# A tuned decoder layer: the norms' factors reach all partitions through device memory instead of an fp32 product with ones

## The chip, the cores and the metric

The kernel runs on one core of a Trainium2 chip. The metric is the device time of one execution in microseconds (us), lower is better. Each kernel is run several times, and the median stands for it; a profile shows one execution. Engines are named as in the profile: PE is TensorE's matrix product and PEld its loading of weights, DVE is VectorE, ACT is ScalarE, POOL is GpSimd, SP is SyncE, which here only issues DMAs.

## The reference

One layer of a hybrid decoder on a batch of one, 256 tokens, width 1024, everything in float32:

```python
h  = rms_norm(x, ln1_g)                       # x * rsqrt(mean(x*x, -1) + 1e-6) * g
q, k, v, z, xbc, dt, ga, gb = split(h @ w_in) # 1024 -> 10272 columns
y_a = moba_attention(rms(q), rms(k), v) @ w_o_attn   # 16 heads of 64; one block of 256: causal attention
y_b = mamba2_mixer(z, xbc, dt, ...) @ w_o_ssm        # conv, chunked scan (2 chunks of 128), 32 heads of 64
x  = x + (sigmoid(ga) * y_a + sigmoid(gb) * y_b) @ w_out
h2 = rms_norm(x, ln2_g)
x  = x + (silu(g_ff) * u_ff) @ w_down         # g_ff, u_ff = split(h2 @ w_gate_up), 2816 wide
h3 = rms_norm(x, ln3_g)
x  = x + (p @ w_ple_proj) * sigmoid(h3 @ w_ple_gate)
```

## The kernel before

**Products.** A float32 product is made of three products of rounded numbers: each operand is split into a high part (`wh` for weights, rounded by ACT) and a residual (`wl` = weight minus high part, by DVE, line 260), and PE computes high times high, high times residual, and residual times high. Weights stream from device memory in pieces of 512 KB, `raw` [128 partitions, 2, 512], all on SP's queue (line 272). There are 5 `raw`, 4 `wh` and 6 `wl` buffers, so a load waits until DVE has read the piece five before it, and DVE runs ahead of PE by at most six residuals.

**Stages.** The input projection runs as panels of 512 columns (`PANELS` gives the order), each 1024 deep: the class `Panel` holds activations as PE's stationary operand, with PSUM tiles `g`; the class `Rows` holds weights as the stationary operand, with tiles `gr`, for the gate and up projections of the feed-forward part. In between stand the attention, the scan, and the output projections. The sequence of the main products is fixed by the code. All else (attention scores, the scan, transposes) is *small work*: its products use PSUM tiles `pb` and are put between the main products.

**What orders the small work.** A `Filler` keeps a count `fill.now` of the nanoseconds of PE work that have been written out so far. Each piece of small work is a generator that yields the earliest count at which its next step may be written; the distances come from the table `LAG`, one number for each kind of step. After each group of main products (three in `Panel.step`) `fill.step()` runs one step that is due. The other engines' instructions follow from this at build time, in an order set by priorities: `w` (weights) ahead of `ev` (evictions) ahead of `bg` (small work). In the trace, each engine then goes through its list in order.

**The norms.** `hn`, `h2n` are normalized activations laid out with the channels on the partitions and the 256 tokens along the row; the factor of a token (`rstd1`, `rstd2`: [128 tokens, 2], made by POOL's power on line 406) is thus needed along the row, the same in every partition. `norm_task` and `norm2` do that: ACT scales the identity by the factor, once for each half of the tokens (`dg`, 2 x [128, 128]); PE multiplies a matrix of ones (`ones_m`) by it in full float32, which leaves in every partition of `pr` the 256 factors; ACT copies them to `rbc`; DVE multiplies by it, four times for the eight blocks of channels: lines 451 and 454 at the first norm, 1139 at the second, where line 1138 first adds the two parts of the residual stream. ACT then rounds the product to the high part, and DVE subtracts for the residual (lines 460 and 1142). The first panels do not need `hn`: they work on activations without the token's factor, which is applied when they are evicted. The gate and up projections need `h2n`.

Elsewhere the kernel already takes one tensor through device memory: `e1t` is written to `e1d` (line 543) and read back, repeated, as `e1c` (line 545).

Of the kernel before, what the change touches and what calls it, by code (L numbers as in the profile page):

```python
# [10 lines left out]
F32 = mybir.dt.float32  # L11
F32R = mybir.dt.float32r
AF = mybir.ActivationFunctionType
ALU = mybir.AluOpType
AX = mybir.AxisListType

P = 128
T = 256
# [16 lines left out]
    ('v', 0, 2048),  # L35
    ('v', 1, 2560),
    ('q', 1, 512),
    ('k', 0, 1024),
    ('k', 1, 1536),
    ('gb', 0, 9248),  # L40
    ('xbc', 4, 7168),
    ('xbc', 5, 7680),
# [23 lines left out]


LAG = {
    "norm": 0, "norm.x": 7982, "norm.k": 5731, "dt": 3113, "dt.t": 1660, "dt.e": 891, "dt.low": 0,
    "dt.end": 5490, "xbc": 3857, "xbc.t": 2999, "xbc.end": 16627, "z": 0, "z.t": 3129, "z.end": 768,  # L70
    "qk": 15739, "qk.t": 6258, "qk.end": 0, "v": 1782, "cb": 3077, "rows": 0, "prep": 877, "seg": 102,
    "seg.next": 9127, "out": 8638, "out.xdt": 352, "out.end": 545, "off": 3241, "off.end": 51, "finish": 4321,
    "finish.ones": 8093, "sc": 1152, "sc.tr": 1416, "tr": 2000, "tr.val": 0, "val": 5094, "val.end": 1076,
    "m": 811, "res": 3010, "ff": 0, "ff.end": 500, "n2": 1163, "n2.rows": 2102, "n2.k": 0, "gu": 0,
}


# [31 lines left out]
def tile_layer(ctx: ExitStack, tc: tile.TileContext, head, xk, pt, vec, w_dt, w_big, w_dn2, w_pp, out):  # L109
    nc = tc.nc  # L110
# [3 lines left out]
    @contextmanager  # L114
    def prio(c):
        saved = tc.cur_priority
        tc.cur_priority = counters[c]
        yield
        counters[c] = tc.cur_priority
        tc.cur_priority = saved  # L120

    const = ctx.enter_context(tc.tile_pool(name="const", bufs=1))
    sb = ctx.enter_context(tc.tile_pool(name="sb", bufs=1))
    psg = ctx.enter_context(tc.tile_pool(name="psg", bufs=4, space=bass.MemoryType.PSUM))
    psb = ctx.enter_context(tc.tile_pool(name="psb", bufs=4, space=bass.MemoryType.PSUM))
    fill = Filler()
    uid = [0]

    def nm(s):
        uid[0] += 1  # L130
        return f"{s}_{uid[0]}"

    def s4(shape, dt=F32):
        return sb.tile([P] + shape, dt, tag="s4", bufs=25, name=nm("s4"))

    def s2(shape, dt=F32):
        return sb.tile([P] + shape, dt, tag="s2", bufs=8, name=nm("s2"))
# [4 lines left out]
    def pb(shape):  # L142
        return psb.tile([P] + shape, F32, tag="b", name=nm("pb"))
# [6 lines left out]
    def act(o, i, f=AF.Copy, **kw):  # L150
        return nc.scalar.activation(o, i, f, **kw)  # L151
# [4 lines left out]
    def queue(ins, main):  # L156


        if fill.last is not None:
            follow(ins, fill.last)  # L160
        if main:
            fill.last = ins
# [6 lines left out]
    def mm(o, lhsT, rhs, start, stop, main=False):  # L169
        ins = nc.tensor.matmul(o, lhsT, rhs, start=start, stop=stop).ins  # L170
        queue(ins, main)
        passes = 4 if lhsT.dtype == F32 else 1
        fill.now += passes * max(107.0, rhs.free_size() / 2.4)
        return ins
# [21 lines left out]
    with prio("w"):  # L196
        zero = nc.const_aps.tensor(0.0, (P, P), F32)
        pw = pb([512])
        for _ in range(7):
            nc.tensor.matmul(pw[:, :P], zero, zero, start=True, stop=True)  # L200
        mhalf = const.tile([P, 16], F32, name="mhalf")
        nc.vector.memset(mhalf, -0.5)
        ones = const.tile([P, 1], F32, name="ones")
        nc.vector.memset(ones, 1.0)
        ident = const.tile([P, P], F32, name="ident")
        make_identity(nc, ident)
        m_tmp = s4([4, P])
        nc.gpsimd.memset(m_tmp[:, 0:3], 1.0)
        ones_m = const.tile([P, P], F32, name="ones_m")
        nc.gpsimd.memset(ones_m, 1.0)  # L210

        nc.gpsimd.affine_select(m_tmp[:, 1], m_tmp[:, 0], pattern=[[-1, P]], compare_op=ALU.is_gt, fill=0.0, base=0, channel_multiplier=1)
        nc.gpsimd.affine_select(m_tmp[:, 2], m_tmp[:, 0], pattern=[[1, P]], compare_op=ALU.is_ge, fill=0.0, base=0, channel_multiplier=-1)
        gt_r = const.tile([P, P], F32R, name="gt_r")
        le_r = const.tile([P, P], F32R, name="le_r")
        nc.gpsimd.tensor_copy(gt_r, m_tmp[:, 1])
        nc.gpsimd.tensor_copy(le_r, m_tmp[:, 2])

        gt1_r = const.tile([P, P], F32R, name="gt1_r")
        nc.gpsimd.memset(m_tmp[0:1, 1], 1.0)  # L220
        nc.gpsimd.tensor_copy(gt1_r, m_tmp[:, 1])
        le_q = const.tile([P, P], F32, name="le_q")
        nc.gpsimd.tensor_scalar(le_q, m_tmp[:, 2], 0.25, None, op0=ALU.mult)

        cmask = const.tile([P, 2, P], F32, name="cmask")
        nc.gpsimd.memset(cmask, 0.0)
        nc.gpsimd.affine_select(cmask[:, 1], cmask[:, 0], pattern=[[-1, P]], compare_op=ALU.is_ge, fill=NEG, base=0, channel_multiplier=1)


    v = const.tile([P, V_N], F32, name="vecs")  # L230
# [179 lines left out]
    rstd1 = const.tile([P, 2], F32, name="rstd1")  # L410
# [23 lines left out]
    def xr_of(k):  # L434
        return xraw[k // 2][:, k % 2] if k else x0[:, 8:]

    def norm_task():
        yield fill.now + LAG["norm"]
        with prio("bg"):
            dg = s2([2, P])  # L440
            for tt in range(2):
                act(dg[:, tt], ident, scale=rstd1[:, tt : tt + 1])
            pr = pb([512])
            mm(pr[:, :T], ones_m, dg.rearrange("p a t -> p (a t)"), True, True)
            rbc = s2([2, T])
            for j in range(2):
                act(rbc[:, j], pr[:, :T])
        for k in range(0, 8, 2):
            with prio("bg"):
                if k:  # L450
                    nc.vector.tensor_mul(xraw[k // 2], xraw[k // 2], rbc)
                else:
                    for j in range(2):
                        nc.vector.tensor_mul(xr_of(j), xr_of(j), rbc[:, 0])
            yield fill.now + LAG["norm.x"]
            with prio("bg"):
                for j in range(k, k + 2):
                    g = g1[:, j : j + 1]
                    act(hn_act[j][0], xr_of(j), scale=g)
                    stt(hn_act[j][1], xr_of(j), g, hn_act[j][0].bitcast(F32), op0=ALU.mult, op1=ALU.subtract)  # L460
            yield fill.now + LAG["norm.k"]
        done.add("norm")
# [6 lines left out]
    e0 = const.tile([P, 32], F32, name="e0")  # L469
    e1t = const.tile([P, P], F32, name="e1t")  # L470
    e1c = const.tile([P, 16, P], F32, name="e1c")
    e1d = ctx.enter_context(tc.tile_pool(name="dram", bufs=1, space=bass.MemoryType.DRAM)).tile([32, P], F32, name="e1d")
    low_h = const.tile([P, P], F32R, name="low_h")
    low_l = const.tile([P, P], F32R, name="low_l")
    done = set()
# [495 lines left out]
    for kind, i, _ in PANELS[2:]:  # L971
# [9 lines left out]
        norm = kind in ("ga", "gb")  # L981
# [96 lines left out]
    rstd2 = const.tile([P, 2], F32, name="rstd2")  # L1078
# [14 lines left out]
    ff = []  # L1093
# [26 lines left out]
    def norm2():  # L1120

        yield fill.now + LAG["n2"]
        with prio("bg"):
            dg = s2([2, P])
            for tt in range(2):
                act(dg[:, tt], ident, scale=rstd2[:, tt : tt + 1])
        yield fill.now + LAG["n2.rows"]
        with prio("bg"):
            pr = pb([512])
            mm(pr[:, :T], ones_m, dg.rearrange("p a t -> p (a t)"), True, True)  # L1130
            rbc = s2([T])
            act(rbc, pr[:, :T])
        for k in range(0, 8, 2):
            yield fill.now + LAG["n2.k"]
            th, tl = (res2.tiles[k // 4][m][:, k % 4 : k % 4 + 2] for m in range(2))
            with prio("bg"):
                t = s2([2, T])
                nc.vector.tensor_add(t, th.bitcast(F32), tl.bitcast(F32))
                nc.vector.tensor_tensor(t, t, rbc.unsqueeze(1).to_broadcast([P, 2, T]), op=ALU.mult)
                h = s4([2, 2, T], F32R)  # L1140
                act(h[:, :, 0], t)
                nc.vector.tensor_sub(h[:, :, 1], t, h[:, :, 0].bitcast(F32))
            h2n.extend(h[:, j].rearrange("p a t -> p (a t)") for j in range(2))

    def rows_gu(i):
# [23 lines left out]
        return after  # L1169

    fill.spawn(norm2(), 0)
    pair(res2.acts, evac_gu)
    h2 = res2.acts[0] + res2.acts[1]
# [104 lines left out]
```

## Time and profile before

| | before |
|---|---|
| median of 3 runs | 584.73 us (584.73, 584.73, 586.01) |
| the profiled execution, whole | 585.25 us |
| its span in the trace | 583.5 us |
| granted clock of TensorE | 1.00 |
| PE, PEld, DVE, ACT, POOL busy | 99%, 84%, 78%, 64%, 8% of the span |
| bytes moved by DMA | 104.97 MB, 180 GB/s on the mean |

The table is made of the page's first lines. Busy shares are means over the whole span; a stage can look different. The span runs from the first to the last recorded instruction; the time of an execution is a little longer, here by 1.75 us. In rows of the trace, the first number is the start in us, the second the duration, and what stands in brackets is the idle time of the engine before it and what ended it. "x2" counts instructions put together in one row.

### The profile page before, as it was taken

To read this page: it belongs to the slowest core of one execution; us is meant where nothing else is said; L and a number is where in the kernel's file an instruction comes from. 1 tells how busy PE (TensorE), PEld (TensorE's weight loads), DVE (VectorE), ACT (ScalarE), POOL (GpSimd) and SP (SyncE) were. 2 spreads that over 40 slices of the span, in tenths; PEclk is the share of its full clock that TensorE was granted. 3 is DMA by queue.
4 is the path that set the end of the run, shared out by engine and by line. 5 is a ranking of instruction groups with operands and counts; after the bars stand their busy time and mean duration, and the time that the engine had idled before them with its cause. 6 is when DMAs were issued, how large, how long until landed. Compare 5 with 4: busy or idle time off the path is not lost.

```text
span 583.5 us, 8612 instructions
## 1 busy us (share of the span) xinstructions
PE 578.3 (99%) x3119; PEld 490.9 (84%) x3119; DVE 457.7 (78%) x745; ACT 373.1 (64%) x582; POOL 47.4 (8%) x44
## 2 busy tenths in 40 slices
PE   9999999999999999999999999999999999999997
PEld 8888888888888888888888888888888888888886
DVE  5686889998998998998898765897777777546464
ACT  7874678676997668666644345766667567535452
POOL 2003100220000311151101000000000000000000
PEclk9999999999999999999999999999999999999999
DMA  8956455476345424435546575555546646565521
GB/s 314 372 188 223 149 182 189 168 194 225 118 154 181 145 79 140 145 111 181 181 144 198 202 258 176 179 181 192 183 163 206 205 153 208 198 202 181 184 71 72
DMA packets 33322, 104.97 MB, mean 180 GB/s; under 512 B 3616, under 2 KB 7040, under 8 KB 33280
## 3 DMA queue, kind: packets, MB, share of 16 engines
q1 hardware_dynamic: 32992, 104.16, 52.9%
q8 instruction: 24, 0.39, 0.3%
q10 hardware_dynamic: 288, 0.26, 0.2%
q14 instruction: 18, 0.15, 0.1%
HBM read 103.28 MB, written 1.06 MB: 179 GB/s over the span
## 4 chain that ended last, share of the span: by engine, by line
PE 99%; DMA 0%; ACT 0%; DVE 0%; issue 0%
PE g L170 52%; PE gr L170 36%; PE pb L170 7%; PE pb L192 3%; DMA x<-in_head 0%; ACT s L151 0%; DVE s L1199 0%; DVE s L1200 0%; ACT wh L151 0%
## 5 line engine op out<-in xcount | busy, mean ns | idle before, releaser
L260 DVE TENSOR_TENSOR wl<-raw,wh 128x1024 fp32r<-128x1024 f32 (+2 forms) x193 | 230.8, 1203 | 90.9 <-ACT wh L151 89.7
L170 PE MATMUL g<-wh,s 128*128 128x512 f32 (+1 forms) x900 | 282.5, 391 | 0.2 <-ACT wh L151 0.2
L151 ACT ACTIVATE wh<-raw 128x1024 fp32r<-128x1024 f32 (+2 forms) x193 | 198.4, 1037 | 131.6 <-PE g L170 81.5
L170 PEld LDWEIGHTS g<-wh,s 128*128 128x128 f32 x900 | 168.8, 189 | 34.7 <-issue 0.5
L170 PE MATMUL gr<-s,wh 128*128 128x512 f32 x608 | 193.5, 399 | 0.0
L170 PE MATMUL g<-wl,s 128*128 128x512 f32 (+1 forms) x450 | 173.3, 387 | 0.0
L170 PEld LDWEIGHTS gr<-s,wl 128*128 128x128 f32 x608 | 114.2, 188 | 26.9
L170 PE MATMUL gr<-s,wl 128*128 128x256 f32 x608 | 119.9, 278 | 0.0
L170 PEld LDWEIGHTS g<-wl,s 128*128 128x128 f32 x450 | 84.4, 188 | 16.4
L170 PEld LDWEIGHTS gr<-s,wh 128*128 128x128 f32 x608 | 93.5, 189 | 1.5 <-issue 0.5
L151 ACT ACTIVATE s<-s 128x512 f32<-128x512 f32 (+2 forms) x49 | 36.6, 747 | 25.4 <-DVE s L1161 15.6
L151 ACT ACTIVATE s<-gr 128x512 f32<-128x512 f32 x76 | 44.3, 592 | 4.2 <-PE gr L170 2.2
L711 POOL TENSOR_SCALAR_AFFINE_SELECT rr<-a_h 128x512 fp32r<-128x512 f32 x16 | 23.8, 1508 | 159.1 <-PE pb L170 118.6
L151 ACT ACTIVATE s<-pb 128x512 f32<-128x512 f32 (+3 forms) x50 | 24.0, 515 | 18.2 <-PE pb L170 12.5
L574 DVE SCALAR_TENSOR_TENSOR s<-s,vecs,s 128x255 f32<-128x255 f32 (+2 forms) x72 | 33.1, 500 | 0.1
L170 PE MATMUL pb<-s,s 128*64 128x128 f32 (+4 forms) x288 | 31.3, 302 | 0.0
L170 PEld LDWEIGHTS pb<-s,s 128*64 128x64 f32 (+1 forms) x288 | 24.7, 154 | 3.9 <-issue 1.2
L192 PE MATMUL pb<-ident,s 128*128 128x128 f32 x170 | 25.0, 273 | 0.0
L406 POOL TENSOR_TENSOR rstd<-tiny,mhalf 128x2 f32<-128x2 f32 x3 | 2.1, 707 | 261.9 <-DVE tiny L405 242.2
L192 PEld LDWEIGHTS pb<-ident,s 128*128 128x128 f32 x170 | 20.3, 141 | 3.0 <-DVE wl L260 0.4
L151 ACT ACTIVATE s<-s,vecs 128x256 f32<-128x256 f32 (+1 forms) x40 | 20.1, 556 | 0.1
L151 ACT ACTIVATE s<-s,tiny,fq 128x128 f32<-128x128 f32 (+1 forms) x32 | 17.1, 537 | 2.0 <-DVE tiny L856 2.0
(146 smaller groups left out, 341.6 us busy)
## 6 DMA issues: line engine op xcount, KB each, us to landing
raw<-in_w_big SPq DMA_DIRECT2D x176, 512.0 KB
raw<-in_head SPq DMA_DIRECT2D x4, 512.0 KB
s<-in_xk SPq DMA_DIRECT2D x4, 512.0 KB
raw<-in_head SPq DMA_DIRECT2D x7, 256.0 KB
e1c<-e1d SPq DMA_DIRECT2D x2, 512.0 KB
raw<-in_w_pp SPq DMA_DIRECT2D x2, 512.0 KB
raw<-in_w_dn SPq DMA_DIRECT2D x2, 512.0 KB
out<-s SPq DMA_DIRECT2D x3, 256.0 KB
```

Of the source, the lines that this page charges most:

```text
L151: return nc.scalar.activation(o, i, f, **kw)
L170: ins = nc.tensor.matmul(o, lhsT, rhs, start=start, stop=stop).ins
L192: queue(nc.tensor.transpose(o, i, ident[: i.shape[0], : i.shape[0]]).ins, False)
L260: nc.vector.tensor_sub(wl, raw, wh.bitcast(F32))
L406: nc.gpsimd.tensor_tensor(dst, t, mhalf[:, : ss.shape[-1]], op=ALU.pow)
L574: stt(cc[:, sft:], u[:, b, : T - sft], cw[3 - sft], cc[:, sft:], op0=ALU.mult, op1=ALU.add)
L711: nc.gpsimd.affine_select(r, bcast(a_h[:, c, h0 : h0 + 4].bitcast(F32), P), pattern=[[0, 4], [1, P]], compare_op=ALU.is_ge, fill=0.0, base ...
```

## The change

A helper `spread(dst, col, n)` takes the place of the scaled identity, the product with ones and the copies. It issues two DMAs on SP's queue: the factors [128, 2] go to row `n` of a small tensor `rows_d` in device memory (256 numbers, one piece of 4 bytes each, since they come from 128 partitions and are transposed on the way); then these 256 numbers are read back into every partition, as `rbc`. At the first norm they are repeated once more along the row (256 KB in all), at the second not (128 KB). The framework makes the read wait for the landing of the write, and DVE's multiply for the landing of the read. The constant `ones_m` and its memset go. The order of the two panels of `k` is swapped, and most numbers of `LAG` are others.

```diff
 PANELS = [
...
     ('q', 1, 512),
+    ('k', 1, 1536),
     ('k', 0, 1024),
-    ('k', 1, 1536),
     ('gb', 0, 9248),
...
 LAG = {
-    "norm": 0, "norm.x": 7982, "norm.k": 5731, "dt": 3113, "dt.t": 1660, "dt.e": 891, "dt.low": 0,
...
-    "m": 811, "res": 3010, "ff": 0, "ff.end": 500, "n2": 1163, "n2.rows": 2102, "n2.k": 0, "gu": 0,
+    "norm": 2000, "norm.x": 7982, "norm.k": 5429, "dt": 3500, "dt.t": 3631, "dt.e": 4000, "dt.low": 0,
...
+    "m": 0, "res": 3010, "ff": 8243, "ff.end": 792, "n2": 1355, "n2.rows": 4311, "n2.k": 2458, "gu": 8000,
 }
...
+    dram = ctx.enter_context(tc.tile_pool(name="dram", bufs=1, space=bass.MemoryType.DRAM))
+    rows_d = dram.tile([2, 2, P], F32, name="rows_d")
...
-        ones_m = const.tile([P, P], F32, name="ones_m")
-        nc.gpsimd.memset(ones_m, 1.0)
...
+    def spread(dst, col, n):
+
+        nc.sync.dma_start(rows_d[n].rearrange("t p -> p t"), col)
+        nc.sync.dma_start(dst, rows_d[n : n + 1].rearrange("n t p -> n (t p)").unsqueeze(1).to_broadcast([P] + list(dst.shape[1:])))
+
     def norm_task():
         yield fill.now + LAG["norm"]
         with prio("bg"):
-            dg = s2([2, P])
-            for tt in range(2):
-                act(dg[:, tt], ident, scale=rstd1[:, tt : tt + 1])
-            pr = pb([512])
-            mm(pr[:, :T], ones_m, dg.rearrange("p a t -> p (a t)"), True, True)
             rbc = s2([2, T])
-            for j in range(2):
-                act(rbc[:, j], pr[:, :T])
+            spread(rbc, rstd1, 0)
...
         yield fill.now + LAG["n2"]
         with prio("bg"):
-            dg = s2([2, P])
-            for tt in range(2):
-                act(dg[:, tt], ident, scale=rstd2[:, tt : tt + 1])
+            rbc = s2([1, T])
+            spread(rbc, rstd2, 1)
         yield fill.now + LAG["n2.rows"]
-        with prio("bg"):
-            pr = pb([512])
-            mm(pr[:, :T], ones_m, dg.rearrange("p a t -> p (a t)"), True, True)
-            rbc = s2([T])
-            act(rbc, pr[:, :T])
         for k in range(0, 8, 2):
...
-                nc.vector.tensor_tensor(t, t, rbc.unsqueeze(1).to_broadcast([P, 2, T]), op=ALU.mult)
+                nc.vector.tensor_tensor(t, t, rbc.to_broadcast([P, 2, T]), op=ALU.mult)
```

Three places in the order of instructions matter below. A row is one instruction: line, operation, what it writes, what it reads, shape; numbers in names tell buffers and uses apart and differ between the kernels.

The first is SP's list at the first norm. Before:

```order
L272 DMA raw_466<-in_w_big 128x1024
L272 DMA raw_472<-in_w_big 128x1024
L272 DMA raw_506<-in_w_big 128x1024
L272 DMA raw_512<-in_w_big 128x1024
L272 DMA raw_560<-in_w_big 128x1024
L272 DMA raw_566<-in_w_big 128x1024
```

And now, with the write (line 439) and the read (line 440):

```order
L272 DMA raw_460<-in_w_big 128x1024
L272 DMA raw_466<-in_w_big 128x1024
L439 DMA rows_d<-rstd_204 128x2x1
L272 DMA raw_500<-in_w_big 128x1024
L272 DMA raw_506<-in_w_big 128x1024
L440 DMA s_55_321<-rows_d 128x2x256
L272 DMA raw_553<-in_w_big 128x1024
L272 DMA raw_559<-in_w_big 128x1024
```

`raw_466` and `raw_472` of before are `raw_460` and `raw_466` now. The write stands between the second and the third of these loads and the read between the fourth and the fifth, so that two weight loads lie between write and read.

The second is DVE's list at the second norm, from one residual to the third after it (`wl_816` is the kernel's 123rd residual, `wl_828` the 125th). Before:

```order
L260 TENSOR_TENSOR wl_816_3964<-raw_814_3962,wh_815_3963 128x1024
L1011 SCALAR_TENSOR_TENSOR s4_788_3851<-pb_794_3877,vecs_104,s4_787_3850 128x256
L1011 SCALAR_TENSOR_TENSOR s4_788_3851<-pb_795_3889,vecs_104,s4_787_3850 128x256
L260 TENSOR_TENSOR wl_825_4012<-raw_823_4010,wh_824_4011 128x1024
L1138 TENSOR_TENSOR s2_809_3950<-s4_772_3785,s4_773_3786 128x512
L1138 TENSOR_TENSOR s2_817_3971<-s4_772_3785,s4_773_3786 128x512
L1138 TENSOR_TENSOR s2_819_3980<-s4_787_3850,s4_788_3851 128x512
L1138 TENSOR_TENSOR s2_821_3989<-s4_787_3850,s4_788_3851 128x512
L1139 TENSOR_TENSOR s2_809_3950<-s2_809_3950,s2_808_3945 128x512
L1139 TENSOR_TENSOR s2_817_3971<-s2_817_3971,s2_808_3945 128x512
L260 TENSOR_TENSOR wl_828_4018<-raw_826_4016,wh_827_4017 128x1024
```

Now, where `wl_810` is the 123rd residual and `wl_818` the 125th:

```order
L1010 SCALAR_TENSOR_TENSOR s4_786_3845<-pb_793_3883,vecs_105,s4_785_3844 128x256
L260 TENSOR_TENSOR wl_810_3948<-raw_808_3946,wh_809_3947 128x1024
L1132 TENSOR_TENSOR s2_811_3973<-s2_811_3973,s2_804_3925 128x512
L1132 TENSOR_TENSOR s2_819_4003<-s2_819_4003,s2_804_3925 128x512
L1010 SCALAR_TENSOR_TENSOR s4_786_3845<-pb_792_3871,vecs_105,s4_785_3844 128x256
L1010 SCALAR_TENSOR_TENSOR s4_786_3845<-pb_793_3883,vecs_105,s4_785_3844 128x256
L260 TENSOR_TENSOR wl_815_3984<-raw_813_3982,wh_814_3983 128x1024
L1135 TENSOR_TENSOR s4_812_3976<-s2_811_3973,s4_812_3976 128x2x256
L1131 TENSOR_TENSOR s2_821_4021<-s4_785_3844,s4_786_3845 128x512
L1135 TENSOR_TENSOR s4_820_4006<-s2_819_4003,s4_820_4006 128x2x256
L260 TENSOR_TENSOR wl_818_3990<-raw_816_3988,wh_817_3989 128x1024
```

The two multiplies by the factors (line 1139 before, 1132 now) stood behind the 124th residual and four adds; they stand ahead of it now, right behind the 123rd. On SP's list there, the write stands behind the load of one `raw` tile, then comes one more load, then the read:

```order
L272 DMA raw_4037<-in_w_big 128x1024
L439 DMA rows_d<-rstd_3627 128x2x1
L272 DMA raw_4043<-in_w_big 128x1024
L440 DMA s_804_3925<-rows_d 128x256
L272 DMA raw_4091<-in_w_big 128x1024
```

In the list of before, the same loads follow each other with nothing between.

The third is DVE's list around its 90th and 91st residual, in the scan. Before, where these are `wl_642` and `wl_645`:

```order
L260 TENSOR_TENSOR wl_642_3151<-raw_640_3149,wh_641_3150 128x1024
L405 TENSOR_SCALAR tiny_617_3048<-pb_616_3045 128x2
L260 TENSOR_TENSOR wl_645_3157<-raw_643_3155,wh_644_3156 128x1024
L734 TENSOR_TENSOR s4_613_3033<-pb_618_3054,dth_210 128x512
L813 TENSOR_TENSOR s4_632_3103<-s4_632_3103 128x512
L821 SCALAR_TENSOR_TENSOR s4_635_3109<-s4_280_1460,vecs_104,s4_634_3108 128x256 x4
L752 TENSOR_TENSOR s2_620_3068<-s2_620_3068,s4_261_1346 128x512
L815 TENSOR_TENSOR s2_633_3106<-s4_632_3103 128x256
L752 TENSOR_TENSOR s2_622_3076<-s2_622_3076,s4_261_1346 128x512
L260 TENSOR_TENSOR wl_654_3201<-raw_652_3199,wh_653_3200 128x1024
L260 TENSOR_TENSOR wl_657_3207<-raw_655_3205,wh_656_3206 128x1024
```

Now, where they are `wl_644` and `wl_647`:

```order
L260 TENSOR_TENSOR wl_633_3105<-raw_631_3103,wh_632_3104 128x1024
L809 TENSOR_TENSOR s4_278_1454<-s4_278_1454,s4_417_2131 128x1024
L405 TENSOR_SCALAR tiny_605_3012<-pb_604_3009 128x2
L733 TENSOR_TENSOR s4_601_2997<-pb_606_3018,dth_211 128x512
L751 TENSOR_TENSOR s2_618_3050<-s2_618_3050,s4_259_1336 128x512
L751 TENSOR_TENSOR s2_620_3058<-s2_620_3058,s4_259_1336 128x512
L260 TENSOR_TENSOR wl_644_3155<-raw_642_3153,wh_643_3154 128x1024
L812 TENSOR_TENSOR s4_621_3077<-s4_621_3077 128x512
L820 SCALAR_TENSOR_TENSOR s4_624_3083<-s4_278_1454,vecs_105,s4_623_3082 128x256 x4
L814 TENSOR_TENSOR s2_622_3080<-s4_621_3077 128x256
L260 TENSOR_TENSOR wl_647_3161<-raw_645_3159,wh_646_3160 128x1024
L260 TENSOR_TENSOR wl_656_3225<-raw_654_3223,wh_655_3224 128x1024
```

The steps of the scan on lines 734 and 752 and of its output norm on lines 813, 815 and 821 (now 733, 751, 812, 814 and 820) stood behind the 91st residual and stand ahead of it now. Over the whole kernel about a quarter of the small products have another place between the main ones, in 140 groups now, 134 before.

More of the change, by code (lines that the diff above doesn't have):

```diff
@@ L68 @@
 LAG = {
-    "norm": 0, "norm.x": 7982, "norm.k": 5731, "dt": 3113, "dt.t": 1660, "dt.e": 891, "dt.low": 0,
[L70 to L73, printed above, removed]
-    "m": 811, "res": 3010, "ff": 0, "ff.end": 500, "n2": 1163, "n2.rows": 2102, "n2.k": 0, "gu": 0,
+    "norm": 2000, "norm.x": 7982, "norm.k": 5429, "dt": 3500, "dt.t": 3631, "dt.e": 4000, "dt.low": 0,
+    "dt.end": 2376, "xbc": 3537, "xbc.t": 3422, "xbc.end": 16627, "z": 12, "z.t": 2127, "z.end": 768,
+    "qk": 15218, "qk.t": 6545, "qk.end": 1000, "v": 0, "cb": 3878, "rows": 145, "prep": 1016, "seg": 184,
+    "seg.next": 7840, "out": 8638, "out.xdt": 527, "out.end": 185, "off": 0, "off.end": 73, "finish": 8000,
+    "finish.ones": 12780, "sc": 1194, "sc.tr": 0, "tr": 1658, "tr.val": 1955, "val": 5094, "val.end": 4010,
+    "m": 0, "res": 3010, "ff": 8243, "ff.end": 792, "n2": 1355, "n2.rows": 4311, "n2.k": 2458, "gu": 8000,
 }
@@ L471, in tile_layer @@
     e1c = const.tile([P, 16, P], F32, name="e1c")
-    e1d = ctx.enter_context(tc.tile_pool(name="dram", bufs=1, space=bass.MemoryType.DRAM)).tile([32, P], F32, name="e1d")
+    e1d = dram.tile([32, P], F32, name="e1d")
     low_h = const.tile([P, P], F32R, name="low_h")
```

## The prediction

> **What bounds the kernel now.** First the page: the span, the busy shares, and the engines' shares of the chain that ended last.
>
> ```profile
> span 583.5 us, 8612 instructions
> PE 578.3 (99%) x3119; PEld 490.9 (84%) x3119; DVE 457.7 (78%) x745; ACT 373.1 (64%) x582; POOL 47.4 (8%) x44
> PE 99%; DMA 0%; ACT 0%; DVE 0%; issue 0%
> ```
>
> TensorE is busy for 99% of the span and makes up 99% of the chain. Whether it ever stands is told by the list of waits, taken for PE alone (time, count, longest):
>
> ```profile
> PE pb L200 <- PEq L1267: 0.8, 1, 0.8
> PE g L170 <- ACT wh L151: 0.2, 1, 0.2
> ```
>
> So after its start TensorE waits 0.2 us in all. A microsecond on another engine is worth nothing unless it makes TensorE stand; a microsecond of TensorE's own work is worth itself. The chain, followed in time, runs through both products that the change removes:
>
> ```profile
> 32.59 0.43 PE pb L170 x2
> 376.79 0.43 PE pb L170 x2
> ```
>
> **The change, part by part.**
>
> *The two fp32 products go.* Their price is read in the timeline of PE, from the starts of the main products around them:
>
> ```profile
> 31.51 0.39 PE L170 MATMUL g<-wl,s 128*128 128x512 f32 x1
> 32.19 0.40 PE L170 MATMUL g<-wl,s 128*128 128x512 f32 x1
> 32.43 0.59 PE L170 MATMUL pb<-s,ones_m 128*128 128x256 f32 x2
> 33.32 0.39 PE L170 MATMUL g<-wl,s 128*128 128x512 f32 x1
> 376.16 0.39 PE L170 MATMUL g<-wl,s 128*128 128x512 f32 x1
> 377.29 0.40 PE L170 MATMUL g<-wl,s 128*128 128x512 f32 x1
> ...
> L170 PE MATMUL pb<-s,ones_m x4: 378/378/379, 32.4 to 376.8; 128*128 128x256 f32 x4
> ```
>
> A group of three main products repeats every 32.19 − 31.51 = 0.68 us; with the fp32 product in it, 33.32 − 32.19 = 1.13 us, and 377.29 − 376.16 = 1.13 us the second time. Each costs 0.45 us (the chain says 0.43). Both: −0.90 us. The four records of 378 ns, added without their overlap, would be 1.51 us, which I keep as the most that can go.
>
> *Work of other engines that goes.*
>
> ```profile
> L151 ACT ACTIVATE s<-ident,rstd x4: 396/400/407, 26.7 to 370.9; 128x128 f32<-128x128 f32 x4
> 33.06 0.66 ACT L151 ACTIVATE s<-pb 128x256 f32<-128x256 f32 x2 [1.87 <-PE pb L170]
> ```
>
> ACT loses 4 × 0.40 for scaling the identity, 0.66 for the two copies from PSUM, and one such copy at the second norm (about 0.33): 2.6 us. The memset of ones at the start goes too. TensorE waits for ACT 0.2 us in the whole span, so I value this at 0, at most 0.2.
>
> *First norm.* The rows now go from rstd1 to device memory and back, both on SP's queue. Before:
>
> ```profile
> 24.04 0.73 POOL L406 TENSOR_TENSOR rstd<-tiny,mhalf 128x2 f32<-128x2 f32 x1 [19.73 <-DVE eps L427]
> 26.97 0.33 SPq L272 DMA_DIRECT2D raw<-in_w_big  x1
> 29.64 0.33 SPq L272 DMA_DIRECT2D raw<-in_w_big  x1
> 33.47 0.43 DVE L454 TENSOR_TENSOR x<-x,s 128x256 f32<-128x256 f32 x1 [1.03 <-ACT s L151]
> ```
>
> rstd1 is there at 24.77. The write stands ahead of the weight load that was issued at 26.97, the read behind the one of 29.64; these two loads wait for buffers, so a write at 24.8 holds up nothing, and the read goes out at about 30.0. No row shows a store of 4-byte pieces. The nearest are the kernel's other round trip through device memory (e1d) and the last output store:
>
> ```profile
> 113.84 0.35 SPq L543 DMA_DIRECT2D e1d<-e1t  x1
> 118.36 1.34 SPq L545 DMA_DIRECT2D e1c<-e1d  x2
> SPq L545 <- DMA e1d<-e1t: 4.2, 1, 4.2
> L1201 SPq DMA_DIRECT2D out<-s x5: 332/332/344, 573.2 to 580.7; - x5
> ```
>
> The e1d write was waited for 4.2 us, and its read went out 118.36 − 113.84 = 4.5 us behind it. The last output store went out at 580.7 and the span ends at 583.5, so it took at most 2.8. Bounds for one transfer: 2.8 to 4.5 us. The read then lands at 32.8 to 34.5, and DVE's multiply, which started at 33.47 before, is late by a microsecond at most. What that may cost is the lead of the residual weights (DVE's wl tiles, which TensorE consumes): instructions on wl tiles, counted from the start to a given time; columns PE, PEld and DVE with counts:
>
> ```profile
> 0.00:42.55 42.55, 20.39 (x56) 10.31 (x56) 20.23 (x21) 1.00 0.80 292
> 0.00:45.60 45.60, 21.99 (x61) 11.25 (x61) 21.78 (x23) 1.00 0.81 291
> ```
>
> The 21st residual is made by 42.55; TensorE begins with it (its 61st product on a residual) just ahead of 45.60. The lead is 3 us, so even a read that lands at 37 costs nothing: 0.
>
> *Second norm.* This is the closest place. Before:
>
> ```profile
> 368.70 0.70 POOL L406 TENSOR_TENSOR rstd<-tiny,mhalf 128x2 f32<-128x2 f32 x1 [52.52 <-DVE tiny L405]
> 370.80 4.28 SPq L272 DMA_DIRECT2D raw<-in_w_big  x2
> 373.50 1.23 DVE L260 TENSOR_TENSOR wl<-raw,wh 128x1024 fp32r<-128x1024 f32 x1 [0.92 <-ACT wh L151]
> 374.64 0.87 DVE L1011 SCALAR_TENSOR_TENSOR s<-pb,vecs,s 128x256 fp32r<-128x256 f32 x2
> 379.47 1.28 DVE L1139 TENSOR_TENSOR s<-s,s 128x512 f32<-128x512 f32 x2
> 383.01 0.68 DVE L1142 TENSOR_TENSOR s<-s,s 128x512 fp32r<-128x512 f32 x1
> 387.52 1.06 ACT L151 ACTIVATE wh<-raw 128x1024 fp32r<-128x1024 f32 x1 [0.71 <-ACT s L151]
> 0.00:381.95 381.95, 183.75 (x632) 118.67 (x633) 148.27 (x125) 1.00 0.55 184
> 0.00:384.90 384.90, 185.42 (x637) 119.49 (x637) 149.49 (x126) 1.00 0.55 184
> ```
>
> rstd2 is there at 369.40 and the write goes out at once. The read follows the load issued at 370.80 and the landing of the write, that is at 372.2 to 373.9, and lands at 375.0 to 378.4 (2 × 2.8 and 2 × 4.5 behind 369.4). By its new place DVE comes to the multiply right behind its 123rd residual, which ends at 374.73: it stands w = 0.3 to 3.7 us with everything behind it. From 374.73 + w: two multiplies 1.28, two evictions 0.87, the 124th residual 1.22, subtract, add, subtract 3 × 0.68, the 125th residual 1.22, which makes 381.4 + w. Before, the 125th was made by 381.95, and TensorE begins with it (its 637th) at about 384.8; 0.45 earlier without the first product: 384.35. The lead left is 3.0 − w: 2.7 to −0.7 us. I take 0, since all but the last fifth of that interval of w is covered; to be kept: 0.7. SP stands too: it holds the read until the write has landed, and the weight loads behind the read come out later. The first of them went out at about 374.75 (the second of the two loads whose issue ended at 370.80 + 4.28 = 375.08) and is rounded by ACT at 387.52, and 12 us of lead hide a delay of a few microseconds: 0.
>
> The Trainium skill ("DMA: Bandwidth & Descriptors", Specifications) says that transfers under 512 bytes make the DMA engine read, modify and write, and its Rules for kernel authors that a non-contiguous last dimension becomes one descriptor for each element; that speaks against a write of 256 pieces of 4 bytes, and by it the write would be the slow half of the pair. By that rule the pair would lie at the upper end or past it; no row here shows a store of this form.
>
> *Moved small work.* The table of delays moves about a quarter of the small products, and with them DVE's evictions. The tightest place is DVE's 91st residual:
>
> ```profile
> 0.00:278.55 278.55, 129.38 (x493) 92.42 (x493) 106.82 (x91) 1.00 0.54 181
> 0.00:283.60 283.60, 132.13 (x501) 93.92 (x501) 107.66 (x92) 1.00 0.54 182
> 278.44 0.68 DVE L734 TENSOR_TENSOR s<-pb,dth 128x512 f32<-128x512 f32 x1
> 282.76 2.36 DVE L260 TENSOR_TENSOR wl<-raw,wh 128x1024 fp32r<-128x1024 f32 x2
> 262.00:268.00 6.00, 6.00 (x58) 4.70 (x55) 4.23 (x6) 3.49 (x6) 2.91 (x2) 1.00 0.08 28
> ```
>
> It is made by 278.5 and wanted at 283.6, a lead of 5.0. Now the small work that stood behind it (278.44 to 282.76, 4.3 us) stands ahead: 0.7 is left, and up to 1.8 more, as DVE stood idle 6.00 − 4.23 = 1.77 us just before (last row, DVE's 4.23 of 6 us busy) and can take the work there. Taken: 0; bounds 0 to 2, if other work is moved there too. Swapping the two panels of k costs nothing: their tiles and products are of one shape. Six more groups of small products between the main ones (140 for 134): I take 0.02 each, the difference of cadence and chain above, 0.1.
>
> *Sum.* −0.90 + 0 + 0 + 0 + 0.1 = −0.8 us. The profiled execution took 585.25 (span 583.5 and 1.75 around it) and would become 584.45. The median of the runs is 584.73, so I forecast 583.9, 0.14% faster. A measurement of this kernel tells about 0.3% (1.75 us) from nothing: below 582.98 is faster, above 586.48 slower.
>
> **The rivals.**
>
> *The round trip at the second norm is late (slower).* The read's packets queue behind one weight load of 512 KB, which takes 2.85 us at the 184 GB/s of the row above, and both transfers take 4.5: 11.85 us. DVE would stand until 381.25, the 125th residual comes 3.5 us too late, and TensorE stands that long: 587.4. It costs from a pair of 8.3 us on (374.73 + 3.0 − 369.4), decides the sign (against −0.8) from 9.1, and makes the kernel slower by 0.3% from 10.9. For it: the pieces of 4 bytes, and the 4.5 us of e1d. Against: the DMA queues are 0.55 busy on the mean up to there, so the read seldom finds a full load ahead of it. Chance 0.13 for a pair over 8.3, of which 0.09 past 10.9.
>
> *The moved small work eats the lead of the 91st residual.* 2 us of standing: 585.9. Against: 1.77 us of idle time ahead of it. Chance 0.08, with 0.03 past 586.48 where it meets other lost leads.
>
> *The products cost nothing.* If TensorE's ends are modelled and the products hide in its queue, their removal gives 0: 584.7. Against: the starts are 1.13 apart in place of 0.68 at both places. Chance 0.07. The Trainium skill ("Perfetto Trace Analysis", Identifying the Most-Contended Engine) says that busy matmul time is a poor measure because matmuls are pipelined, and that the share of weight loading is better; that is 84% here. By that rule TensorE has slack and the time would stay at 584.7; the waits, 0.2 us after the start, do not show such slack.
>
> *More goes than the products.* All 1.51 us of the four records and the 0.2 of waiting: 583.0. Chance 0.04 to go below that.
>
> *The change does only half of what it says* (the products go, and the table of delays moves nothing that TensorE waits for): −0.9 or −0.8, which is the forecast again, since I cost the table at nothing.
>
> **How the numbers follow.** Forecast as told, with the table's part or without it, 0.68, DMA late 0.13, moved work 0.08, products free 0.07, more 0.04. The range is 583.0 (everything removed) to 586.4 (a pair of 10.8 us, or moved work with a little on top). Faster 0.04; slower 0.09 + 0.03 = 0.12; same 0.84.
>
> **What would show it.** In the new profile: no products on ones_m, and starts 0.68 apart at both places; PE busy about 577.4. Waits of PE still under 0.5 us; a wait of PE for a wl tile near 384 is the first rival, near 283 the second. DVE waits on the read's landing at the second norm, not at the first; SP shows a wait for the write's landing twice, each of 2.5 to 4.5 us. Wrong if the pair takes over 8.3 us, if the write of 4-byte pieces holds up the weight loads behind it, or if the delays make TensorE stand in a place I took for covered.

## The result, and the profile after

The changed kernel takes 594.08 us (median of 5, 593.61 to 595.14), the kernel before 584.79 beside it (584.73 to 587.96): a ratio of 1.0148, 95% interval 1.0129 to 1.0167. It is 9.3 us slower, where the forecast was 583.9 and the range ended at 586.4. The profiled execution has a span of 591.9 us, 8.4 more than before.

The same lines of the page, of the changed kernel:

```profile
span 591.9 us, 8600 instructions
PE 580.0 (98%) x3115; PEld 490.2 (83%) x3115; DVE 456.1 (77%) x745; ACT 370.5 (63%) x575; POOL 44.2 (7%) x43
PE 87%; DMA 8%; DVE 3%; issue 1%; ACT 1%; POOL 0%; SPq 0%; DVEq 0%
```

TensorE's share of the chain has fallen from 99% to 87%, and DMA now holds 8% of it: 4.7% for the new write and read, the rest for loads at the start, through which the chain now runs. The waits of PE (time, count, longest), where before there were the 0.8 us of the start and 0.2:

```profile
PE g L172 <- DVE wl L260: 5.2, 4, 2.3
PE g L172 <- ACT wh L153: 1.5, 3, 1.2
PE pb L202 <- PEq L1260: 0.8, 1, 0.8
```

Which DMA is in the chain is told by its pieces in order of time (start, length, what):

```profile
26.35 9.40 DMA rows_d<-rstd
35.77 6.71 DMA s<-rows_d
375.32 7.09 DMA rows_d<-rstd
382.43 4.27 DMA s<-rows_d
```

The write of 1 KB takes 9.4 us at the first norm and 7.1 at the second, the read 6.7 and 4.3. DVE's timeline shows the end of both pairs, by the idle time in brackets:

```profile
42.50 0.42 DVE L453 TENSOR_TENSOR x<-x,s 128x256 f32<-128x256 f32 x1 [4.77 <-DMA s<-rows_d]
386.78 1.29 DVE L1132 TENSOR_TENSOR s<-s,s 128x512 f32<-128x512 f32 x2 [6.21 <-DMA s<-rows_d]
```

The pair is 42.50 − 26.35 = 16.2 us, and 386.78 − 375.32 = 11.5. Behind these multiplies stand the next residuals in DVE's list. In ACT's list, the rounding of the multiplied activations at the first norm stands ahead of the next high part `wh`, so that one is late too:

```profile
42.96 0.51 ACT L153 ACTIVATE s<-x 128x256 fp32r<-128x256 f32 x1 [5.84 <-DVE x L453]
44.71 1.04 ACT L153 ACTIVATE wh<-raw 128x1024 fp32r<-128x1024 f32 x1
```

PE's timeline shows it standing, first for that high part and then for residuals:

```profile
45.81 0.49 PE L172 MATMUL g<-wh,s 128*128 128x512 f32 x1 [1.17 <-ACT wh L153]
48.56 0.50 PE L172 MATMUL g<-wl,s 128*128 128x512 f32 x1 [2.26 <-DVE wl L260]
390.05 0.50 PE L172 MATMUL g<-wl,s 128*128 128x512 f32 x1 [1.03 <-DVE wl L260]
392.99 0.50 PE L172 MATMUL g<-wl,s 128*128 128x512 f32 x1 [1.28 <-DVE wl L260]
```

The standing is not all. In this profile PE is busy 580.0 us, 1.7 more than before with less to do. The windows behind the first standing show why (the third number from the right is the granted clock, then DMA share and GB/s):

```profile
48.00:50.00 2.00, 1.44 (x4) 1.16 (x5) 2.00 (x4) 2.00 (x4) 0.00 (x0) 0.76 0.13 51
50.00:52.00 2.00, 2.00 (x6) 1.54 (x5) 2.00 (x3) 0.84 (x1) 0.00 (x0) 0.50 0.74 221
52.00:54.00 2.00, 2.00 (x9) 1.62 (x9) 1.82 (x4) 0.60 (x1) 1.61 (x1) 0.89 0.75 211
```

By these windows the clock is halved for about 3.4 us, and the loss is 2 × 0.24 + 2 × 0.50 + 2 × 0.11 = 1.7 us of work. To add it up, take the start of the same main product in both traces, after minus before: the difference grows by 0.93 us near 17 us, falls by 0.45 where the first product with ones was, grows by 5.58 at the first norm (3.43 standing, 1.7 of halved clock, the rest in starting again, since products that follow each other overlap: 0.39 us long, 0.23 apart), falls by 0.19 until 376, falls by 0.45 at the second product, grows by 2.88 at the second norm (2.31 standing, the rest in starting again), and changes by −0.03 from there: 8.27 at the last product. The 0.93 lies ahead of the change, in the first weights; the same point stands at −0.6 to +0.4 in the profiles of the experiments, so it is put down to this execution.

### The profile page after: what moved, and what is told of

Read it like the earlier page. It is cut to its first block, busy times and chain, and to the rows that moved or that the text cites. A ratio compares the mean times of both kernels' runs of the same rounds, so it can differ in the third digit from the quotient of the medians.

```text
span 591.9 us, 8600 instructions
## 1 busy us (share of the span) xinstructions
PE 580.0 (98%) x3115; PEld 490.2 (83%) x3115; DVE 456.1 (77%) x745; ACT 370.5 (63%) x575; POOL 44.2 (7%) x43
## 4 chain that ended last, share of the span: by engine, by line
PE 87%; DMA 8%; DVE 3%; issue 1%; ACT 1%; POOL 0%; SPq 0%; DVEq 0%
PE g L172 42%; PE gr L172 36%; PE pb L172 6%; PE pb L194 3%; DMA rows_d<-rstd 3%; DMA s<-rows_d 2%; DMA s<-in_xk 2%; DMA raw<-in_head 1%; DVE wl L260 1%; ACT s L153 1%; DVE xraw L450 0%; DVE s L1010 0%; POOL rstd L406 0%; DVE s L459 0%; DVE s L1132 0%
## 5 line engine op out<-in xcount | busy, mean ns | idle before, releaser
L710 POOL TENSOR_SCALAR_AFFINE_SELECT rr<-a_h 128x512 fp32r<-128x512 f32 x16 | 21.1, 1337 | 155.1 <-PE pb L172 114.4
L153 ACT ACTIVATE s<-g 128x512 f32<-128x512 f32 x24 | 13.5, 590 | 6.3 <-PE g L172 5.4
```

The lines of the kernel that those rows point to most:

```text
L710: nc.gpsimd.affine_select(r, bcast(a_h[:, c, h0 : h0 + 4].bitcast(F32), P), pattern=[[0, 4], [1, P]], compare_op=ALU.is_ge, fill=0.0, base ...
```

## The experiments

Two theories stood at first. *The trip*: all of the loss comes from the two DMAs being long, and the rest of the change behaves as forecast. *The table*: the moved small work makes PE stand. To part them, the trip was taken out, and table and trip were each put alone. A fourth kernel keeps the long trip and moves DVE's multiplies back in its list. The expectations on record number the residuals one lower than the text ahead of the prediction; outside of them, that text's count is used here. By it the changed kernel's multiplies stand behind the 19th and the 123rd residual.

**The change without the trip.** POOL fills `rbc` in place. The kernel leaves out the spreading, so each partition's row holds that partition's own factor, and its output is not the layer's. The first multiplies stand behind the 17th residual. In the code below, `...` stands for lines, or parts of a line, that are not shown.

```diff
-    "norm": 2000, "norm.x": 7982, ...
+    "norm": 2000, "norm.x": 5000, ...
...
+    def near(dst, col):
+        for j in range(dst.shape[1]):
+            ptt(dst[:, j], col[:, 0:1].to_broadcast([P, T]), col[:, 0:1].to_broadcast([P, T]), op=ALU.add)
...
-            spread(rbc, rstd1, 0)
+            near(rbc, rstd1)
+        yield fill.now + 14000
...
-            spread(rbc, rstd2, 1)
+            near(rbc, rstd2)
```

> The changed kernel without the trip through device memory: POOL fills the rows in place from the factors (so each row holds its own partition's factor, summed twice, instead of the 256 factors; the spreading is left out), and DVE's first multiplies stand behind the 16th residual. Theory 'the trip' (all of the loss comes from how long the two DMAs take, and the rest of the change behaves as forecast): PE no longer waits after its start (under 1 us in all), the granted clock stays at 1.00, and the time is 583.9 (584.79 - 0.90 + 0.1), between 583.2 and 585. Rival 'the table' (the moved small work makes PE stand): it stays at 590 or more, with PE waits of several us.

583.97 us, ratio 0.9981 (0.997 to 0.9991) to 585.17 beside it: 1.1 us faster by the ratio, where −0.8 was forecast. Its only waits of PE are the start's 0.8 and one of 0.3 near it. Products, ACT's work and the moved small work together cost and brought what the sum said, within 0.3 us; the loss comes with the trip.

**Table alone, and trip alone.** The first is the kernel before with the new `LAG` and `PANELS`, the second the changed kernel with the old ones.

> The kernel before with only the new table of delays and the new order of the two panels; the products with ones stay. Theory 'the trip': the moved small work costs nothing, 584.8, between 584.2 and 585.8. Rival 'the table': 590 or more; a smaller loss of 1 to 2 us would say that the lead of the 91st residual was eaten.

> The changed kernel's trip through device memory under the old table of delays and the old order of panels. Theory 'the trip': the loss stays, as DVE meets its multiplies at the same residuals (behind the 18th and the 122nd): write 9 us and read 6 to 7 at the first norm, together 11 or more at the second, PE stands 3 to 4 us and 2 to 4 us; 592 to 597. Rival 'the table': back at about 584.

The table alone: 584.95, ratio 0.9994 (0.9982 to 1.0005), no change. The trip alone: 597.54, ratio 1.0206 (1.0187 to 1.0225), slower still than the change and just above the range expected: PE stood 5.3 us at once at the first norm, for activations that ACT rounds, and its clock was halved after both norms. The theory of the table falls.

**The multiplies moved back.** The other multiplies by the factors are ordered like the one shown, each behind the newest residual (`newest`) that the program has written so far.

```diff
             spread(rbc, rstd1, 0)
+        yield fill.now + 30000
...
-    "norm": 2000, "norm.x": 7982, "norm.k": 5429, ...
+    "norm": 2000, "norm.x": 1000, "norm.k": 5429, ...
...
-    ... "n2": 1355, "n2.rows": 4311, "n2.k": 2458, ...
+    ... "n2": 1355, "n2.rows": 12500, "n2.k": 500, ...
...
+                    follow(nc.vector.tensor_mul(xraw[k // 2], xraw[k // 2], rbc).ins, newest[0])
```

> The changed kernel with DVE's multiplies moved back in its list: the first two behind the 22nd residual (made after 43 us), the second norm's behind the 126th. The trip itself is unchanged. Theory 'place' (the trip is long but only the multiply that stands ahead of residuals makes PE stand): the pair of DMAs still takes about 16 and 11 us, DVE waits under 1 us for its landing, PE under 1 us, and the time is 583.9 to 585. Rival 'stalled loads' (the write of 4-byte pieces itself holds up the weight loads so long that residuals come late): PE still stands 1 to 4 us near 45 or 385, with ACT waiting for weight loads; 587 to 591.

590.2, ratio 1.0081 (1.0065 to 1.0096): within the rival's range, but not for the rival's reason. Its longest waits of PE, besides the start's:

```profile
PE gr L172 <- DVE s L1104: 2.4, 2, 2.1
PE g L172 <- DVE s L462: 0.7, 2, 0.5
PE gr L172 <- DVE s L1138: 0.5, 1, 0.5
```

PE no longer waits for a residual or a weight load at 45 or 385. It waits 0.5 us at 395 for normalized activations (L1138) and 2.1 us at 399 for an eviction (L1104) that stands behind more of them in DVE's list: the second norm's multiplies had been moved too far. Behind the 2.1 us the clock was halved again. So the move was repeated with the second norm's multiplies behind the 125th residual instead of the 127th:

> The changed kernel's 256 pieces of 4 bytes with the first multiplies behind the 22nd residual and the second norm's behind the 124th (in place of the 126th, where the gate and up products had to wait for the normalized activations). Theory 'place': the pair still takes 16 and 12 us, PE stands under 1.5 us in all, the clock stays at 1.00, 584.2 to 586. Rival 'stalled loads': weight loads behind the write are late, PE stands 2 us or more and its clock is halved for a while, 587 to 591.

584.92, ratio 1.0 (0.9989 to 1.001). The writes were no shorter (11.7 and 7.0 us), and PE stood at neither norm. In the profiled execution, which at 588.13 was the slowest of its twelve, PE stood at a third place, where a small product waited 2.0 us for DVE's work on q and k, and its clock fell again. In this profile a long trip costs nothing at the norms once no residual that is wanted soon stands behind it; as a median the kernel is only as fast as the kernel before, so a place free of all other cost was not found by hand.

**What makes the trip long.** Two theories: *queue*, write and read wait behind weight loads on SP's queue; *pieces*, the many small writes are slow in themselves. One kernel moves both DMAs to POOL's queue (`nc.gpsimd.dma_start`), two write larger pieces, and one makes three trips behind the last store.

> The changed kernel with write and read on POOL's queue instead of SP's; the weight loads stay on SP's, so they no longer stand behind write and read in one queue. Theory 'pieces' (256 pieces of 4 bytes are written one after the other, about 0.45 us each on every one of 16 DMA engines, and hold up whatever those engines carry): the write still takes 6 to 8 us, the pair 10 or more, PE stands, 590 to 595. Rival 'queue' (write and read are long because they wait behind weight loads in SP's queue): write 2.8 to 4.5, read under 4.5, pair under 8.3, and the time falls to 584 to 585.

595.36, ratio 1.0177 (1.0157 to 1.0196). On a queue of its own the write takes as long:

```profile
POOL s L440 <- DMA rows_d<-rstd: 17.2, 2, 8.7
```

That is 8.6 us for each write on the mean, counted from the end of its issue. The theory of the queue falls. Quiet trips:

```diff
+            flat = end_d[n : n + 1].rearrange("n t p -> n (t p)")
...
+            if n == 0:
+                nc.sync.dma_start(end_d[n].rearrange("t p -> p t"), tcol[:, 0:2])
+            elif n == 1:
+                nc.sync.dma_start(end_d[n].rearrange("t p -> (t p)").rearrange("(p t) -> p t", t=2), back[:, 0:2])
+            else:
+                nc.sync.dma_start(flat, back[0:1, :])
...
+            nc.sync.dma_start(back, flat.to_broadcast([P, T]))
```

> The changed kernel with three more trips behind its last store, when no other DMA is left, each of 1 KB to device memory and a read of it into all partitions, each waiting for the one before: first as 256 pieces of 4 bytes, then as 128 pieces of 8 bytes, then as one piece of 1 KB from one partition. The span grows by their sum. Theory 'pieces': write to landing 6 to 8 us for the first, 3 to 5 for the second, 2 to 3 for the third; the reads alike at 2 to 3. Rival 'queue': the three writes alike, 2 to 3 us each.

SP's timeline gives issue after issue; each waits for the landing of the one before:

```profile
592.13 0.39 SPq L1208 DMA_DIRECT2D end_d<-e  x1
599.81 0.33 SPq L1214 DMA_DIRECT2D back<-end_d  x1
604.69 0.32 SPq L1210 DMA_DIRECT2D end_d<-back  x1
607.55 0.32 SPq L1214 DMA_DIRECT2D back<-end_d  x1
611.52 0.24 SPq L1212 DMA_DIRECT2D end_d<-back  x1
612.63 0.34 SPq L1214 DMA_DIRECT2D back<-end_d  x1
```

Writes: 599.81 − 592.13 = 7.7 us for pieces of 4 bytes, 2.9 for 8 bytes, 1.1 for one piece; reads 4.9 and 4.0. The first of these still met the end of the last output store, sent just before it; with nothing else at all under way the same write took 7.71 us (the last price below). So the write of the change is slow by itself. At the first norm it also nearly stops the other traffic; windows of the changed kernel while its first write is under way (clock, DMA share, GB/s; a packet is counted in the window it starts in):

```profile
26.00:28.00 2.00, 1.00 1.02 408
30.00:32.00 2.00, 1.00 0.38 21
32.00:34.00 2.00, 1.00 0.60 18
34.00:36.00 2.00, 1.00 0.45 18
37.00:38.00 1.00, 1.00 0.93 279
```

From 408 GB/s the core falls to about 20 for 6 us, with two weight loads on the way, issued at 27.84 and 30.52; ACT stood 3.3 us for one of them, until 35.4. The prediction had said that a write there holds up nothing. At the second norm, with one load issued behind the write, the traffic did not stop: 140 and 213 GB/s in the windows 376 to 378 and 378 to 380. Larger pieces in the layer, first 128 pieces of 8 bytes, which DVE's multiplies then read in the order that this leaves, the multiplies at the same residuals as in the change:

```diff
-        nc.sync.dma_start(rows_d[n].rearrange("t p -> p t"), col)
+        nc.sync.dma_start(rows_d[n].rearrange("t p -> (t p)").rearrange("(p t) -> p t", t=2), col)
```

> The changed kernel with the factors written as 128 pieces of 8 bytes (both factors of a partition together); DVE's multiplies read the rows in the order that this leaves, and the second norm's are two of 256 columns in place of one of 512. Theory 'pieces', by number of pieces: the write takes 4 to 6 us, the pair 11 to 12 at the first norm and 8 to 9 at the second, PE stands under 1.5 us in all, 584 to 587. Rival 'bytes or queue': as the changed kernel, 593 to 596.

Then two pieces of 512 bytes, after a transpose on PE and a copy by ACT; in this kernel the second norm's multiplies stand behind the 125th residual:

```diff
-        nc.sync.dma_start(rows_d[n].rearrange("t p -> p t"), col)
+        pt_ = pb([512])
+        transpose(pt_[:2, :P], col)
+        rw = s2([P])
+        act(rw[:2], pt_[:2, :P])
+        nc.sync.dma_start(rows_d[n], rw[:2])
```

> The changed kernel with the factors [128, 2] transposed by PE to [2, 128] and copied by ACT first, so that the write is two pieces of 512 bytes; the build then puts the second norm's multiplies behind the 124th residual. Theory 'pieces': the write takes 2.5 to 4.5 us, holds up no load, DVE waits under 2 us at each norm, PE under 0.5 us; two transposes on PE cost 0.1 to 0.3 us each, so 584.79 - 0.9 + 0.5 = 584.4, between 583.8 and 585.6. Rival 'queue': pair still above 10 us, 588 or more.

8 bytes: 585.17, ratio 1.0007 (0.9998 to 1.0017); write 5.9 and 3.4 us. Two rows: 584.54, ratio 0.9996 (0.9986 to 1.0007); write 2.6 and 1.7 us. Both are as fast as the kernel before: the loss is gone with the small pieces, the gain of 0.8 us that was forecast is not reached.

**Number of pieces, or their neighbourhood.** The quiet prices do not go by number: halving it took 7.7 us to 2.9. So the number, the size and the distance in device memory were varied in seven more quiet writes, each followed by a read of one number that waits for its landing.

> The changed kernel with seven more writes behind its last store, when no other DMA is left, each followed by a read of one number that waits for its landing: (1) 256 pieces of 4 bytes, packed as in the change; (2) 128 pieces of 4 bytes, packed; (3) 256 pieces of 4 bytes, each 64 bytes from the next; (4) the same, 512 bytes from the next; (5) 128 pieces of 8 bytes, packed; (6) 128 pieces of 8 bytes, 64 bytes from the next; (7) as (1) again. Price: from the issue of the write to the issue of its read. Theory 'number' (each piece costs the same): 7 to 8 us for (1), (3), (4) and (7), about 4 for (2), 3 for (5) and (6). Rival 'neighbours' (pieces that several DMA engines write into the same short stretch of device memory wait for each other): 7 to 8 for (1) and (7), 4 or more for (2), but under 3.5 for (3) and (4), and (6) no longer than (5).

SP's timeline, a write (`price<-pcol`) and its read by turns:

```profile
588.70 0.39 SPq L1212 DMA_DIRECT2D price<-pcol  x1
596.34 0.25 SPq L1215 DMA_DIRECT2D pback<-price  x1
599.49 0.34 SPq L1210 DMA_DIRECT2D price<-pcol  x1
606.41 0.24 SPq L1215 DMA_DIRECT2D pback<-price  x1
609.60 0.37 SPq L1212 DMA_DIRECT2D price<-pcol  x1
611.16 0.23 SPq L1215 DMA_DIRECT2D pback<-price  x1
612.49 0.37 SPq L1212 DMA_DIRECT2D price<-pcol  x1
614.05 0.23 SPq L1215 DMA_DIRECT2D pback<-price  x1
615.42 0.34 SPq L1208 DMA_DIRECT2D price<-pcol  x1
618.97 0.24 SPq L1215 DMA_DIRECT2D pback<-price  x1
620.42 0.33 SPq L1208 DMA_DIRECT2D price<-pcol  x1
621.84 0.24 SPq L1215 DMA_DIRECT2D pback<-price  x1
623.16 0.37 SPq L1212 DMA_DIRECT2D price<-pcol  x1
630.87 0.24 SPq L1215 DMA_DIRECT2D pback<-price  x1
```

In order: 256 packed pieces of 4 bytes 7.64 us; 128 packed pieces of 4 bytes 6.92; 256 pieces of 4 bytes 64 bytes apart 1.56; 512 bytes apart 1.56; 128 packed pieces of 8 bytes 3.55; the same 64 bytes apart 1.42; the first again 7.71. The theory of the number falls. Pieces of 4 bytes that lie 64 bytes apart are nearly as cheap as one row of 1 KB (1.56 us against 1.1); packed, 256 of them cost five times as much. Distances between 8 and 64 bytes were not tried. What the memory or the DMA engines do with such neighbours no trace shows; that they wait for each other is a reading that fits, and not shown.

**The first norm's multiplies behind the 21st residual, with pieces of 8 bytes.**

> The 128 pieces of 8 bytes again, with the first norm's multiplies moved back in DVE's list, from behind the 18th to behind the 20th residual; the second norm's stay behind the 122nd. Theory 'place': the 0.9 us for which PE stood goes, and with both products gone the time is 584.98 - 0.9 + 0.2 = 584.3, between 583.7 and 584.9, faster than before by 0.1%. Rival: the loads that the write holds up come late wherever the multiplies stand, 585.2 as without the move.

585.65, ratio 1.0012 (1.0004 to 1.0021): a miss. The standing at the first norm is gone, and a transpose in the small work waits 1.0 us for ACT at 135 instead. The delays of the first norm's later steps were changed with the move; that they cause this wait is likely and was not tried by itself.

**A version that is faster than both.** DVE turns the factors, which stand in the first 2 of 32 columns of `wide`, into rows by one transpose of 32 x 32 blocks. The write is then 8 pieces of 128 bytes in four DMAs:

```diff
+        rw = s2([32])
+        nc.vector.transpose(rw, wide[n])
+        for b in range(0, P, 32):
+            nc.sync.dma_start(rows_d[n][:, b : b + 32], rw[b : b + 2])
```

> The changed kernel, with the factors turned into rows by one DVE transpose of 32 x 32 blocks ahead of the write (no work on PE); the write is then 8 pieces of 128 bytes in four DMAs, and nothing else is placed by hand. Theory 'neighbours' (only pieces that share a short stretch of device memory are slow): write 1.5 to 3 us, the pair 6 to 7.5, both covered, PE under 0.3 us of waits and the clock at 1.00, so the time is that of the kernel without the trip: 584.0, between 583.6 and 584.7, faster than before by 0.05 to 0.25%. Rival: the read alone, 4 to 5 us behind weight loads, still makes DVE stand at the second norm and residuals late, 585 or more.

583.84, ratio 0.9976 (0.9967 to 0.9985) to 585.39 beside it: 1.4 us faster than the kernel before by the ratio. The forecast's sum was −0.8, and the kernel without the trip gained 1.1; what the rest of the 1.4 is was not looked into, so the time's nearness to 583.9 is in part luck. PE waits 0.8 us and 0.4 at the start and nowhere else. SP's timeline at the two norms:

```profile
25.04 1.20 SPq L445 DMA_DIRECT2D rows_d<-s  x4
29.43 0.38 SPq L446 DMA_DIRECT2D s<-rows_d  x1
370.00 1.17 SPq L445 DMA_DIRECT2D rows_d<-s  x4
373.30 0.35 SPq L446 DMA_DIRECT2D s<-rows_d  x1
```

At the second norm the read goes out 3.3 us behind the first of the four writes, and DVE waits 0.6 us for its landing and starts at 376.45. That is a pair of 6.5 us, inside the bounds of 5.6 to 9.0 (twice 2.8 and twice 4.5) on which the forecast was built.

## Why the prediction was wrong, point by point

- *The products.* Right: −0.45 us each, at both places in the trace. The rival by which they cost nothing falls with it.
- *Other engines' work, the panels, the moved small work at 283 us.* Right: without the trip 583.97, and table and panels alone without effect. PE did not stand near 283.
- *The step that failed: "Bounds for one transfer: 2.8 to 4.5 us".* The write took 9.4 and 7.1. The bounds came from a write of 32 rows of 512 bytes (e1d) and from an output store, and were carried over to 256 packed pieces of 4 bytes, whose quiet price alone is 7.7. So the pair, put at 5.6 to 9.0, took 16.2 and 11.5. The prediction had said that no row shows such a store, and took the nearest rows for bounds all the same. The upper end of a cost that no row shows should have been left far higher.
- *The reads.* Too low at the first norm alone: 6.7 us, behind two weight loads that the write had held up. At the second it took 4.3, inside the bounds; in quiet the reads of 128 KB took 4.9 and 4.0.
- *The lead.* Right at the second norm, incomplete at the first. At the second it was said that a pair over 8.3 us costs its excess; the pair of 11.5 cost 2.9 (11.5 − 8.3 = 3.2). At the first a landing at 37 was said to cost nothing; it came at 42.5, 5.5 later, and PE stood 3.4. Of these, 1.2 were for a high part of ACT's, whose place behind the rounding of the multiplied activations the prediction did not count.
- *The rival "the round trip is late"* was the true case: DVE stands, residuals come late, PE stands. It was priced for the second norm alone and with 0.13 for its chance. Its pair of 11.85 us is close to the 11.5 by luck, since it was made of 4.5 for the write, 2.85 behind a load and 4.5 for the read, where 7.1 and 4.3 were measured. Two things were missing from it: the first norm, and the halved clock.
- *The Trainium skill* ("DMA: Bandwidth & Descriptors", Specifications) had warned of transfers under 512 bytes; the pieces of 4 bytes spoke for the rival, but the bounds of the sum were left as they were. Its direction agrees with 7.7 us against 1.1 here; as a rule of size alone it does not hold, since pieces of 4 bytes took 1.56 us when 64 bytes apart.

## What to carry to other kernels

A DMA's price is not read from its bytes: before a small store is put on a path, look how many pieces it has and how close they land, and if no row of the trace shows that form, let the upper bound of its cost be large or measure it behind the last store. When a wait is added on an engine that also feeds TensorE, the lead of what stands behind it is the allowance; here it was read right to 0.3 us at the second norm, and missed the work of a second engine (ACT) behind the same wait at the first. Turning the column into rows on DVE first cost less here than letting the DMA do it: a pair of 6.5 us against 11.5 at the second norm.

## What was not expected of the hardware

- Packed pieces of 4 bytes: 7.6 us for 256, 6.9 for 128; 64 bytes apart 1.56 for 256. Packed pieces of 8 bytes: 2.9 to 3.6 for 128.
- While 256 packed pieces of 4 bytes landed at the first norm, the core moved about 20 GB/s instead of 408. With the write on POOL's queue and the loads on SP's it was 14 to 49 between 28 and 34 us, instead of 407. At the second norm the traffic went on.
- The granted clock was halved after short standings: 1.96 us (the multiplies behind the 125th residual) and 2.1 us (behind the 127th) were enough; two standings of 1.03 and 1.28 us with work between were not. It then stayed halved for 3.4 us or twice as long (6.8 us at the second norm with the trip on POOL's queue). The Trainium skill ("TensorE: Matmul & The Clock Gate", Part 1) gives an idle window of about 3.4 us before the clock falls, and the same length for its return; the return agrees where it took 3.4 us, the fall came sooner here.
